# A weight's high and low part issued as two pieces of an issue model

## The chip, the cores and the metric

The kernel runs on one core of one Trainium2 chip. The metric is the device time of one execution in microseconds; the time before is the median of three runs. One further execution was recorded by the hardware profiler, and all durations below come from it.

## The reference

The reference is a small decoder trunk: two layers, each a half-step feed-forward block, a token mixer and a second half-step feed-forward block, with RMS norms before and after each. The input x is 256 tokens of 1024 values, all in float32.

```python
D_MODEL, SEQ, DEPTH, D_FF = 1024, 256, 2, 2816

def swiglu(x, w_gu, w_down):
    g, u = jnp.split(x @ w_gu, 2, axis=-1)
    return (jax.nn.silu(g) * u) @ w_down

def hybrid_mixer(h, w_in, w_out, ...):
    proj = h @ w_in
    pa, pb, pc = jnp.split(proj, [2 * A_WIDTH, 2 * A_WIDTH + B_IN], axis=-1)
    gate_a, rec_a = jnp.split(pa, 2, axis=-1)
    rec = causal_dwconv(rec_a, lru_conv_w, lru_conv_b)
    ya = rg_lru(rec, ...) * jax.nn.gelu(gate_a)      # sigmoid gates, a scan along the tokens
    yb = ssd_mixer(pb, ...)                          # decay matrices in chunks of 128 tokens
    yc = chunk_sgu(pc, ...)                          # gelu, layer norm, a 128 x 128 mixing matrix, a product
    return jnp.concatenate([ya, yb, yc], axis=-1) @ w_out
```

Nearly all of the arithmetic is in the products with the weights; the mixer has many small steps beside them.

## The kernel before

**Matmuls in three passes.** Each float32 operand is held as a high part (rounded to the format fp32r) and a low part (the remainder). A product is high·high, high·low and low·high, all accumulated in the same bank (`mm3`, `b_tile`, `wide_tile`; lines 436, 719 and 742 record the matmuls). The activations are split the same way into nT.

**Weights.** There are 656 weight units of 128 rows and up to 512 columns, used once each in a fixed order and numbered d. SP loads them in chunks of four, about 1 MB, into three buffers named stg (line 356). ACT then writes a unit's high part into a slot (a copy, line 407, or a scaled activation, line 411), and DVE writes the low part, stg minus high (line 408, or line 412 with the scale). There are 17 slots (named s_w in the profile), and a few spare ones of another kind (s_a). A slot comes free when PE has used the unit for the last time. A chunk's buffer comes free when its four low parts are written.

**What sets the order.** The program is written out by a model of time in Python: `T` holds a modelled time for each engine, and PE's is "now". PE's matmuls are issued by the main path. Everything else (evacuations, norms, convolutions, the recurrent unit, the state-space chunks, the gating unit) is a *chain*: a generator that issues one operation when the model finds it due. `Chain.op` (line 138) decides this: an operation that needs the result of another engine is due 0.13 us (`HOP`) after it, and is issued when this is at most 0.7 us (`AHEAD`) ahead of now. `pump` moves the chains that are due and then calls `fill`, which issues weight splits while a slot is free and `fill_time` is not ahead of now: that is the later of the modelled DVE time, the modelled ACT time (each less 0.6, `FILL`) and the arrival of the chunk. One call of `split_next` issues the high on ACT and the low on DVE together, and books the time of both.

Only up to 15 us of modelled time (`PIN`) is this order kept exactly; after that a scheduler places the instructions with the written order as priority. Each engine executes its own instructions in order, so an instruction that waits holds up everything behind it on its engine.

**The places touched by the steps below.** In a feed-forward block, `evac_block` takes the block sums of a row tile through a silu on ACT, a product on DVE and four transposes on PE. In the mixer, `decay` and `decay_group` build the decay matrices (sixteen PE matmuls, twelve exponentials on ACT), `sgu` is the gating unit (gelu on ACT, statistics on DVE, rstd and two products per row tile on POOL, matmuls with wst, transposes with ident), `conv` the convolutions on DVE, `lru_tile` the recurrent gates (matmuls with wbd, sigmoids on ACT), `ssd_chunk` the state-space chunks, and `post` the norm behind a block with the update of x.

Of the kernel before, what the change touches and what calls it, by code (L numbers as in the profile page):

```python
# [8 lines left out]
F32 = mybir.dt.float32  # L9
# [3 lines left out]
ALU = mybir.AluOpType  # L13
# [15 lines left out]
HOP = 0.13  # L29
# [193 lines left out]
class Kernel:  # L223
    def __init__(self, ctx, tc, x, wts, pf, pb, gpost, wst, wri, out):
# [33 lines left out]
        self.next_dma = self.next_split = 0  # L258
        self.wt, self.wh, self.wready, self.slot_time = {}, {}, {}, {}
        self.extra, self.keep_free = 0, 4  # L260
        self.pairs = {}


# [104 lines left out]
    def fill_time(self):  # L368
        d = self.next_split
        ci, _ = self.u2c[d]  # L370
        if self.slot_kind() is None or d < 2 and ("nT", 0, d, 0) not in self.ready:
            return 0.0
        return max(self.T["dve"] - FILL, self.T["act"] - FILL, self.carrive.get(ci, 0.0) - 0.3)

    def fill(self):
        did = False
        while self.next_split < len(self.units):
            d = self.next_split
# [1 line left out]
            while self.next_dma <= min(ci + NSTG - 1, len(self.chunks) - 1):  # L380
                self.dma_chunk()
            kind = self.slot_kind()
            if kind is None or d < 2 and ("nT", 0, d, 0) not in self.ready:
                break
            lead = d - self.cur
            if self.fill_time() > self.now() and (lead > 2 or self.carrive[ci] > self.now() + 0.3):
# [7 lines left out]
    def split_next(self, kind):  # L394
        d = self.next_split
        nc, T = self.nc, self.T
        u = self.units[d]
        w = unit_width(u)
        ci, o = self.u2c[d]
        src = self.ctile[ci][:, o:o + w]  # L400
        t, h = self.get([P, 2, 512], F32R, kind)
        hi, lo = t[:, 0, :w], t[:, 1, :w]
        sc = u[3] is not None
        T["act"] = max(T["act"], self.carrive[ci], self.slot_time.get(h, 0.0) + HOP) + 0.095 + w * 0.000833 + 0.095 * sc
        T["dve"] = max(T["dve"], T["act"] + HOP) + 0.07 + 0.06 * sc + w * 0.00104
        if not sc:
            self.keep(nc.scalar.copy(hi, src))  # L407
            self.keep(nc.vector.tensor_tensor(out=lo, in0=src, in1=hi.bitcast(F32), op=ALU.subtract))  # L408
        else:
            s = self.pcol(u[1], u[3][0], u[3][1])  # L410
            self.keep(nc.scalar.activation(hi, src, AF.Copy, scale=s))  # L411
            self.keep(nc.vector.scalar_tensor_tensor(out=lo, in0=src, scalar=s, in1=hi.bitcast(F32),  # L412
                                                     op0=ALU.mult, op1=ALU.subtract))
        self.wt[d], self.wh[d], self.wready[d] = t, h, T["dve"]
        self.next_split += 1

    def unit(self, d):
        self.cur = max(self.cur, d)
# [847 lines left out]
```

## Time and profile before

| what | value |
|---|---|
| median of 3 runs | 965.46 us (965.22 to 966.49) |
| profiled execution | 964.02 us, span 962.2 us, granted clock 0.998 |
| PE busy | 945.7 us, 98% of the span |
| DVE busy | 701.3 us, 73% |
| ACT busy | 622.8 us, 65% |
| POOL busy | 39.1 us, 4% |
| chain that ended last | PE 88%, DVE 7%, ACT 2% |
| low parts on DVE (lines 412 and 408) | 307.3 + 122.2 us, 623 instructions |
| high parts on ACT (lines 411 and 407) | 285.1 + 107.5 us, 623 instructions |

A row of a timeline gives the start, the time that a group of like instructions took, the engine, the line, the operation, what it writes and reads, the count, and in brackets the idle time before it with what ended it. A row of the table of stages gives a stretch of time, its length, and the busy time of PE, the weight loads of PE (PEld), DVE, ACT and POOL, then the clock, the share of the DMA engines and their rate. The rows of PE's waits give the sum of a wait, how often it came and the longest. Line 138 is the line of `Chain.op`: all chain operations have it, so they are told apart by their tiles.

### The profile page before, as it was taken

The numbers are of one execution on the slowest core, as the hardware profiler recorded it, in microseconds if no ns is written. First come the engines' busy times: TensorE is split into PE (matmuls) and PEld (weight loads), VectorE is DVE, ScalarE is ACT, GpSimd is POOL, SyncE is SP. The second block draws the span as 40 slices with busy tenths as digits, with TensorE's granted clock in tenths as the row PEclk, the third lists the DMA queues.
The fourth block names the chain that finished last, engine by engine and source line by source line (L and its number), as shares of the span: only waits on it lengthen the run. The fifth ranks groups of instructions, "written<-read, shape, count | busy, mean of one in ns | idle before, by whom it ended". The sixth has DMA issues, their size and how long they took to land.

```text
span 962.2 us, 13913 instructions
## 1 busy us (share of the span) xinstructions
PE 945.7 (98%) x5150; PEld 814.4 (85%) x5150; DVE 701.3 (73%) x1313; ACT 622.8 (65%) x1199; POOL 39.1 (4%) x58
## 2 busy tenths in 40 slices
PE   9999999999999999999999999999999999999997
PEld 7888888889987888888888888888999778888885
DVE  4997776566899777776566888666588997787732
ACT  7876665576968676665565666655589686665631
POOL 1100000001001100000010000000010100000000
PEclk9999999999999999999999999999999999999999
DMA  7865565443236755566435455663431564455621
GB/s 259 326 215 198 195 215 203 153 175 111 88 134 220 283 181 197 177 219 223 170 132 196 176 190 205 220 229 114 171 125 49 211 231 188 177 205 195 218 78 44
DMA packets 27140, 175.51 MB, mean 182 GB/s; under 512 B 3008, under 2 KB 3392, under 8 KB 8384
## 3 DMA queue, kind: packets, MB, share of 16 engines
q1 hardware_dynamic: 25200, 169.93, 49.6%
q10 hardware_dynamic: 1872, 4.70, 1.4%
q8 instruction: 40, 0.66, 0.3%
q14 instruction: 28, 0.23, 0.1%
HBM read 173.57 MB, written 1.05 MB: 181 GB/s over the span
## 4 chain that ended last, share of the span: by engine, by line
PE 88%; DVE 7%; ACT 2%; issue 1%; POOL 1%; DMA 0%; SPq 0%; DVEq 0%; POOLq 0%; ACTq 0%
PE acc L742 42%; PE acc L436 39%; PE acc L138 4%; PE acc L719 3%; DVE s_a L138 3%; DVE s_w L412 2%; ACT s_a L138 1%; DVE s_f L138 1%; DVE x L138 1%; POOL postr L138 1%; ACT L138 1%; DMA x<-in_x_dram 0%; ACT junk L138 0%; DVE s_m L138 0%; POOL lnr L138 0%
## 5 line engine op out<-in xcount | busy, mean ns | idle before, releaser
L742 PE MATMUL acc<-nT,s_w 128*128 128x512 f32 x2240 | 395.0, 337 | 0.0
L742 PEld LDWEIGHTS acc<-nT,s_w 128*128 128x128 f32 x2240 | 343.1, 188 | 48.2
L412 DVE SCALAR_TENSOR_TENSOR s_w<-stg,pf,s_w 128x512 fp32r<-128x512 f32 (+2 forms) x439 | 307.3, 735 | 54.3 <-ACT s_w L411 53.9
L411 ACT ACTIVATE s_w<-stg,pf 128x512 fp32r<-128x512 f32 (+2 forms) x439 | 285.1, 702 | 59.0 <-PE acc L436 32.6
L436 PE MATMUL acc<-s_w,s_a 128*128 128x512 f32 x984 | 227.4, 390 | 0.0
L436 PEld LDWEIGHTS acc<-s_w,s_a 128*128 128x128 f32 x984 | 184.4, 188 | 38.1
L408 DVE TENSOR_TENSOR s_w<-stg,s_w 128x512 fp32r<-128x512 f32 x184 | 122.2, 689 | 42.5 <-ACT s_w L407 42.1
L407 ACT CAST s_w<-stg 128x512 fp32r<-128x512 f32 x184 | 107.5, 619 | 52.7 <-PE acc L436 34.6
L436 PE MATMUL acc<-s_w,nT 128*128 128x512 f32 (+1 forms) x522 | 129.6, 395 | 0.8 <-DVE nT L138 0.5
L138 DVE TENSOR_TENSOR s_m<-acc,s_m 128x256 f32<-128x256 f32 (+2 forms) x172 | 71.2, 417 | 66.0 <-ACT s_m L138 61.6
L436 PEld LDWEIGHTS acc<-s_w,nT 128*128 128x128 f32 x522 | 96.0, 190 | 20.8 <-DVE s_w L412 1.5
L138 ACT COPY s_m<-acc 128x256 f32<-128x256 f32 x144 | 52.4, 364 | 83.0 <-PE acc L742 82.9
L719 PE MATMUL acc<-nT,s_w 128*128 128x256 f32 x588 | 76.0, 283 | 0.0
L719 PEld LDWEIGHTS acc<-nT,s_w 128*128 128x128 f32 x588 | 71.5, 188 | 0.3
L436 PE MATMUL acc<-s_w,s_m 128*128 128x512 f32 x192 | 48.0, 399 | 0.0
L436 PEld LDWEIGHTS acc<-s_w,s_m 128*128 128x128 f32 x192 | 35.1, 188 | 7.0
L138 DVE TENSOR_TENSOR s_f<-acc,gp 128x512 f32<-128x512 f32 x24 | 16.5, 687 | 33.3 <-ACT junk L138 33.1
L138 ACT ACTIVATE s_m<-s_m 128x512 f32<-128x512 f32 x36 | 22.7, 629 | 25.1 <-DVE s_m L138 25.1
L138 POOL TENSOR_TENSOR postr<-postv,mhalf 128x1 f32<-128x1 f32 x12 | 9.8, 819 | 693.4 <-DVE postv L138 693.4
L138 ACT ACTIVATE junk<-acc 128x512 bf16<-128x512 f32 x24 | 14.2, 594 | 35.9 <-PE acc L436 35.5
L138 ACT CAST s_a<-s_m 128x512 fp32r<-128x512 f32 x36 | 22.2, 617 | 20.7 <-DVE s_m L138 20.7
L138 DVE SCALAR_TENSOR_TENSOR s_a<-s_f,pf,s_a 128x255 f32<-128x255 f32 (+2 forms) x60 | 29.6, 502 | 4.5 <-ACT s_a L138 4.3
(138 smaller groups left out, 608.6 us busy)
## 6 DMA issues: line engine op xcount, KB each, us to landing
stg<-in_wts_dram SPq DMA_DIRECT2D x146, 1024.0 KB, 4.8
stg<-in_wts_dram SPq DMA_DIRECT2D x12, 768.0 KB, 4.2
stg<-in_wts_dram SPq DMA_DIRECT2D x4, 780.0 KB, 4.2
gp<-in_gpost_dram ACTq DMA_DIRECT2D x6, 512.0 KB, 5.5
stg<-in_wts_dram SPq DMA_DIRECT2D x3, 512.0 KB, 4.2
x<-in_x_dram SPq DMA_DIRECT2D x4, 256.0 KB, 5.1
out_dram<-x SPq DMA_DIRECT2D x4, 256.0 KB, 2.0
pb<-in_pb_dram ACTq DMA_DIRECT2D x2, 265.0 KB, 6.2
```

Source lines behind the costliest of these rows:

```text
L138: ins = fn(*args, **kw)
L407: self.keep(nc.scalar.copy(hi, src))
L408: self.keep(nc.vector.tensor_tensor(out=lo, in0=src, in1=hi.bitcast(F32), op=ALU.subtract))
L411: self.keep(nc.scalar.activation(hi, src, AF.Copy, scale=s))
L412: self.keep(nc.vector.scalar_tensor_tensor(out=lo, in0=src, scalar=s, in1=hi.bitcast(F32), op0=ALU.mult, op1=ALU.subtract))
L436: self.keep(mm(out, a, b, start=start and i == 0, stop=stop and i == 2))
L719: self.keep(self.nc.tensor.matmul(out, a, b, start=k == 0 and i == 0, stop=k == KT - 1 and i == 2))
L742: self.keep(self.nc.tensor.matmul(out, a, x, start=k == 0 and i == 0, stop=k == KT - 1 and i == 1))
```

## The change

The low part of a weight is no longer issued with its high part. `split_next` issues the high as before and adds a chain, `split_low`, that issues the low part by the rule of `Chain.op`: when its high part's modelled end plus 0.13 us is at most 0.7 us ahead of now. The modelled time of DVE is booked only then, and a unit counts as ready only when its low part has been issued. While more than two low parts are outstanding, no further high part is issued.

```diff
     def fill_time(self):
...
-        if self.slot_kind() is None or d < 2 and ("nT", 0, d, 0) not in self.ready:
+        if self.slot_kind() is None or self.lows > 2 or d < 2 and ("nT", 0, d, 0) not in self.ready:
             return 0.0
...
     def fill(self):
...
-            if kind is None or d < 2 and ("nT", 0, d, 0) not in self.ready:
+            if kind is None or self.lows > 2 or d < 2 and ("nT", 0, d, 0) not in self.ready:
                 break
...
     def split_next(self, kind):
...
         T["act"] = max(T["act"], self.carrive[ci], self.slot_time.get(h, 0.0) + HOP) + 0.095 + w * 0.000833 + 0.095 * sc
-        T["dve"] = max(T["dve"], T["act"] + HOP) + 0.07 + 0.06 * sc + w * 0.00104
+        c = Chain(self, T["act"])
+        c.eng = "act"
         if not sc:
             self.keep(nc.scalar.copy(hi, src))
-            self.keep(nc.vector.tensor_tensor(out=lo, in0=src, in1=hi.bitcast(F32), op=ALU.subtract))
+            low = c.tt(w, lo, src, hi.bitcast(F32), ALU.subtract)
         else:
             s = self.pcol(u[1], u[3][0], u[3][1])
             self.keep(nc.scalar.activation(hi, src, AF.Copy, scale=s))
-            self.keep(nc.vector.scalar_tensor_tensor(out=lo, in0=src, scalar=s, in1=hi.bitcast(F32),
-                                                     op0=ALU.mult, op1=ALU.subtract))
-        self.wt[d], self.wh[d], self.wready[d] = t, h, T["dve"]
+            low = c.stt(w, lo, src, s, hi.bitcast(F32), ALU.mult, ALU.subtract)
+        self.add(self.split_low(c, low, d, t, h))
         self.next_split += 1
+
+    def split_low(self, c, low, d, t, h):
+
+        self.lows += 1
+        yield from low
+        self.lows -= 1
+        self.wt[d], self.wh[d], self.wready[d] = t, h, c.t
```

In the changed kernel the lines of the matmuls are 444, 727 and 750, the high parts have lines 409 and 413, and the low parts have line 138 like the other chain operations. Buffer numbers differ between the two programs, since they are given in the order of issue.

**Three places where the order differs.** First ACT in the second feed-forward of layer 1 (about 320 us). Rows that write s_w or s_a from stg are the high parts of weights; the first row is d226 before and d227 after, and the row with acc and rs is the silu of row tile 1. Before:

```order
L411 ACTIVATE s_w_3332<-stg,pf 128x512
L411 ACTIVATE s_w_3338<-stg,pf 128x512
L534 DMA gp<-in_gpost_dram 128x1024
L138 ACTIVATE s_m_3345<-acc_3230,rs_3177 128x512
L411 ACTIVATE s_w_3361<-stg,pf 128x512
L138 COPY s_m_3378<-acc_3350 128x256
L411 ACTIVATE s_w_3387<-stg,pf 128x512
```

After:

```order
L413 ACTIVATE s_w_3335<-stg,pf 128x512
L413 ACTIVATE s_w_3343<-stg,pf 128x512
L413 ACTIVATE s_w_3345<-stg,pf 128x512
L542 DMA gp<-in_gpost_dram 128x1024
L138 ACTIVATE s_m_3350<-acc_3230,rs_3184 128x512
L413 ACTIVATE s_w_3372<-stg,pf 128x512
L413 ACTIVATE s_a_3374<-stg,pf 128x512
```

The silu (s_m with acc_3230) stood behind d227 and now stands behind d229, two high parts later; on DVE the two low parts likewise stand ahead of the product that follows the silu.

Second PE in the first mixer (about 225 us). Rows with later, tri and ad are the sixteen matmuls of `decay_group`; the others are tiles of the projection (`b_tile`). Before:

```order
L719 MATMUL acc_2226<-nT,s_w_2068 128x256 x3
L138 MATMUL acc_2261<-later,ident_r 128x384
L138 MATMUL acc_2261<-tri,ad 128x128 x3
L138 MATMUL acc_2262<-later,ident_r 128x384
L138 MATMUL acc_2262<-tri,ad 128x128 x3
L138 MATMUL acc_2263<-later,ident_r 128x384
L138 MATMUL acc_2263<-tri,ad 128x128 x3
L138 MATMUL acc_2265<-later,ident_r 128x384
L138 MATMUL acc_2265<-tri,ad 128x128 x3
L719 MATMUL acc_2266<-nT,s_w_2076 128x256 x3
```

After:

```order
L727 MATMUL acc_2229<-nT,s_w_2066 128x256 x3
L727 MATMUL acc_2273<-nT,s_w_2075 128x256 x3
L727 MATMUL acc_2273<-nT,s_w_2081 128x256 x3
L727 MATMUL acc_2273<-nT,s_w_2087 128x256 x3
L727 MATMUL acc_2273<-nT,s_w_2094 128x256 x3
L727 MATMUL acc_2273<-nT,s_w_2105 128x256 x3
L727 MATMUL acc_2273<-nT,s_w_2112 128x256 x3
L727 MATMUL acc_2273<-nT,s_w_2118 128x256 x2
L138 MATMUL acc_2299<-later,ident_r 128x384
L138 MATMUL acc_2299<-tri,ad 128x128 x3
L138 MATMUL acc_2307<-later,ident_r 128x384
L138 MATMUL acc_2307<-tri,ad 128x128 x3
```

The decay matmuls began with the next projection tile (acc_2266 before, acc_2273 now) and now begin 20 of its 24 matmuls later. On DVE two low parts (d168 and d169) stand ahead of the decay pieces (nacs, wdt) that feed them.

Third DVE in the same mixer (from about 231 us). bst, bmv, lnv and the TENSOR_SCALAR rows with lnr are the gating unit's layer norm; rows with s_f and pf are convolution pieces; s_w is a low part. Before:

```order
L138 TENSOR_TENSOR s_f_2334<-acc_2266,rb 128x256
L138 BN_STATS bst<-s_a_2043 128x6
L138 BN_STATS bst<-s_a_2143 128x6
L138 BN_AGGR bmv<-bst 128x2 x2
L138 TENSOR_SCALAR lnv<-bmv 128x1 x2
L138 TENSOR_SCALAR s_a_2352<-s_a_2043,bmv,lnr 128x256
L138 TENSOR_SCALAR s_a_2367<-s_a_2143,bmv,lnr 128x256
L138 SCALAR_TENSOR_TENSOR s_a_2333<-s_f_2334,pf,s_a_2333 128x255
L138 SCALAR_TENSOR_TENSOR s_a_2333<-s_f_2334,pf,s_a_2333 128x254
L138 TENSOR_TENSOR s_f_2375<-acc_2336,rb 128x256
L138 SCALAR_TENSOR_TENSOR s_a_2333<-s_f_2334,pf,s_a_2333 128x253
L412 SCALAR_TENSOR_TENSOR s_w_2513<-stg,pf,s_w_2513 128x384
```

After:

```order
L138 TENSOR_TENSOR s_f_2337<-acc_2273,rb 128x256
L138 BN_STATS bst<-s_a_2051 128x6
L138 BN_AGGR bmv<-bst 128x2
L138 SCALAR_TENSOR_TENSOR s_a_2336<-s_f_2337,pf,s_a_2336 128x255
L138 TENSOR_TENSOR s_f_2377<-acc_2340,rb 128x256
L138 SCALAR_TENSOR_TENSOR s_a_2336<-s_f_2337,pf,s_a_2336 128x254
L138 TENSOR_SCALAR lnv<-bmv 128x1
L138 BN_STATS bst<-s_a_2146 128x6
L138 SCALAR_TENSOR_TENSOR s_a_2336<-s_f_2337,pf,s_a_2336 128x253
L138 BN_AGGR bmv<-bst 128x2
L138 SCALAR_TENSOR_TENSOR s_a_2336<-s_f_2377,pf,s_a_2336 128x255
L138 TENSOR_SCALAR lnv<-bmv 128x1
```

The statistics of the second row tile (s_a_2143 before, s_a_2146 now) stood ahead of all convolution pieces and now stand between them; the low part at the end (s_w_2513) has moved further back. The second mixer, at 697 to 774 us, has the same moves.

More of the change, by code (lines that the diff above doesn't have):

```diff
@@ L260, in __init__ @@
         self.extra, self.keep_free = 0, 4
+        self.lows = 0
         self.pairs = {}
```

## The prediction

> **What bounds the kernel now.** I read the busy times first, then what PE waits for over the whole span, then a table of stages. PE rows carry the end of the program:
>
> ```profile
> PE 945.7 (98%) x5150; PEld 814.4 (85%) x5150; DVE 701.3 (73%) x1313; ACT 622.8 (65%) x1199; POOL 39.1 (4%) x58
> PE 88%; DVE 7%; ACT 2%; issue 1%; POOL 1%; DMA 0%; SPq 0%; DVEq 0%; POOLq 0%; ACTq 0%
> ...
> PE acc L138 <- DVE x L138: 3.2, 5, 0.9
> PE acc L138 <- DVE s_a L138: 2.0, 2, 1.0
> PE acc L138 <- ACT s_a L138: 1.0, 2, 0.5
> PE acc L436 <- DVE s_w L412: 0.3, 1, 0.3
> ```
>
> PE is busy 945.7 of 962.2 us, so 16.5 us is all that any order can win. The last row says what the low parts cost PE directly: it waited once for one, 0.3 us. If the change wins, it is not because weights arrive sooner. It is because DVE, on which every low part runs, does other work earlier or later. So I looked for the stages where PE idles (columns: PE busy, PEld, DVE, ACT, POOL, clock, DMA share, GB/s):
>
> ```profile
> 232.00:246.00 14.00, 13.03 (x101) 12.30 (x101) 13.15 (x35) 10.12 (x23) 4.03 (x6) 1.00 0.23 77
> 246.00:262.00 16.00, 15.34 (x129) 14.93 (x129) 13.14 (x35) 15.29 (x33) 0.00 (x0) 1.00 0.19 67
> 285.00:300.00 15.00, 13.79 (x61) 10.48 (x61) 14.27 (x29) 13.19 (x31) 2.29 (x3) 1.00 0.53 193
> ...
> 223.00:300.00 77.00, 74.08 (x496) 66.08 (x495) 67.09 (x153) 62.86 (x139) 8.30 (x11) 1.00 0.35 121
> 697.00:774.00 77.00, 74.00 (x496) 66.03 (x495) 67.00 (x153) 62.70 (x139) 8.28 (x11) 1.00 0.34 121
> ```
>
> The last two rows are the two mixers: PE idles 2.9 us in one and 3.0 us in the other, of which 0.97, 0.66 and 1.21 us lie in the three stages above them, and DVE is busy 13 to 14 us of each 14 to 16. Here DVE's order decides. In the feed-forward stages PE has no idle worth naming, so there a new order can only cost.
>
> **The change part by part.** It adds and removes no instruction: PE, DVE, ACT, POOL and SP issue as many as before, and every DMA stands in its old order. All terms are PE stalls that go or come.
>
> **Two new stalls in the feed-forward stages.** In the second feed-forward of layer 1 the block sums of row tile 1 go ACT (silu), DVE (product), PE (four transposes). The order listing shows that ACT now has the highs of two more weights (d228, d229 of the unit list) ahead of the silu, and DVE their two lows ahead of the product:
>
> ```profile
> 319.72 1.94 ACT L411 ACTIVATE s_w<-stg,pf 128x512 fp32r<-128x512 f32 x3
> 321.56 0.67 ACT L138 ACTIVATE s_m<-acc,rs 128x512 f32<-128x512 f32 x1
> 323.55 0.72 ACT L411 ACTIVATE s_w<-stg,pf 128x512 fp32r<-128x512 f32 x1 [1.32 <-DMA stg<-in_wts_dram]
> ...
> 319.85 2.74 DVE L412 SCALAR_TENSOR_TENSOR s_w<-stg,pf,s_w 128x512 fp32r<-128x512 f32 x4 [2.27 <-ACT s_w L411]
> 322.51 0.68 DVE L138 TENSOR_TENSOR s_m<-acc,s_m 128x512 f32<-128x512 f32 x1
> ...
> 321.63 1.90 PE L742 MATMUL acc<-nT,s_w 128*128 128x512 f32 x10
> 323.61 0.60 PE L138 MATMUL acc<-ident,s_m 128*128 128x128 f32 x4
> ```
>
> The high of d228 cannot start before its DMA lands, 323.55. The x3 row gives 0.61 us from one high to the next, so d229 starts at 324.16, the silu at 324.8, and it ends near 325.5 (0.67). The product (0.68) ends at 326.2 to 326.3. PE's transposes move back by nine matmuls. Eleven matmuls lie between 321.63 and 323.61, 0.18 each, so PE stands there at 323.61 + 1.6 = 325.2. What was free before (the silu done 1.3 us before that DMA) becomes a **stall of about 1.1 us**. The cover was the time in which ACT waited for the DMA; it is gone because the silu now queues behind it.
>
> The same pattern stands at 37 us in the first feed-forward, with a table load on top:
>
> ```profile
> 21.18 1.28 ACT L138 ACT_TABLE_LOAD   x1 [0.40 <-PE acc L436]
> 22.47 0.69 ACT L138 ACTIVATE s_m<-acc,rs 128x512 f32<-128x512 f32 x1
> 30.10 0.72 ACT L411 ACTIVATE s_w<-stg,pf 128x512 fp32r<-128x512 f32 x1 [1.87 <-DMA stg<-in_wts_dram]
> 30.73 1.94 ACT L411 ACTIVATE s_w<-stg,pf 128x512 fp32r<-128x512 f32 x3
> 32.57 0.67 ACT L138 ACTIVATE s_m<-acc,rs 128x512 f32<-128x512 f32 x1
> ...
> 35.72 1.03 PE L138 MATMUL acc<-ident,s_m 128*128 128x128 f32 x8
> ...
> 794.50 0.69 DVE L138 TENSOR_TENSOR s_m<-acc,s_m 128x512 f32<-128x512 f32 x1 [0.25 <-PE acc L436]
> ```
>
> The first silu, and with it the load, moves from 22.47 to behind the high of d23, which ends at 32.57. Then 1.28 for the load, 0.6 for each silu, and three highs (d24 to d26, 0.61 each) end near 37.0; the low of d26 0.66, the product 0.6, so row tile 1 is ready at 38.3. PE's transposes of tile 0 go back four matmuls and those of tile 1 one more: 35.72 + 4 × 0.18 + 0.4 + 0.18 = 37.0. **Stall 1.3 us.** The ready side hangs on the DMA of the weights (the high of d20 waits for it until 30.10 in either order), so whatever PE wins between 16 and 22 us, where the normalization's small steps move ahead of a low, is not added: it is spent here. The second layer has a move of the same kind (last row), but there the silu keeps its place and only two lows pass the product: 794.50 becomes 795.8, two thirds of which PE's own move by four matmuls (0.7) covers; the product had been ready before PE came, and I take no stall. Sum of the feed-forward stages: **+2.4 us**. Bounds: 0, if the DMA lands sooner than before by the 1.1 us, and +4.5, if at both places a further low gets in front of the product's consumer (0.66) and the DMA is as late as PE is early.
>
> **The front of each mixer.** Two lows pass the decay pieces on DVE (224 us), and PE takes the sixteen decay matmuls 20 matmuls of the f-tiles later:
>
> ```profile
> 225.17 0.34 PE L138 MATMUL acc<-later,ident_r 128*128 128x384 f32 x1
> 228.47 8.42 PE L719 MATMUL acc<-nT,s_w 128*128 128x256 f32 x70
> 241.17 0.41 PE L138 MATMUL acc<-ident,s_a 128*128 128x128 f32 x2 [0.97 <-DVE s_a L138]
> ...
> 230.94 1.27 ACT L138 ACTIVATE s_a<-acc,rs 128x512 f32<-128x512 f32 x2
> 243.54 1.28 ACT L138 ACT_TABLE_LOAD   x1
> 244.84 0.47 ACT L138 ACTIVATE s_a<-acc,pf 128x256 f32<-128x256 f32 x1
> ...
> 234.24 3.13 POOL L138 TENSOR_TENSOR s_a<-s_a,pb 128x256 f32<-128x256 f32 x4 [0.16 <-DVE s_a L138]
> ...
> 231.89 0.77 DVE L138 BATCH_NORM_STATS2 bst<-s_a 128x6 f32<-128x256 f32 x2
> 234.44 1.65 DVE L138 SCALAR_TENSOR_TENSOR s_a<-s_f,pf,s_a 128x255 f32<-128x255 f32 x2
> 236.79 1.00 DVE L412 SCALAR_TENSOR_TENSOR s_w<-stg,pf,s_w 128x384 fp32r<-128x384 f32 x1
> 238.10 0.60 DVE L412 SCALAR_TENSOR_TENSOR s_w<-stg,pf,s_w 128x384 fp32r<-128x384 f32 x1
> 251.25 1.00 DVE L138 SCALAR_TENSOR_TENSOR s_a<-s_f,pf,s_a 128x255 f32<-128x255 f32 x2 [1.88 <-ACT s_a L138]
> ```
>
> The x70 row gives 0.12 us a matmul, so 20 of them are 2.3 us: gelu starts at 233.3 instead of 230.94, the statistics at 234.0 instead of 231.89, and POOL's four products (0.78 each) run from about 237.8 to 240.8 instead of 234.24 to 237.4. Against this, the gating unit's matmuls and transposes go back on PE as well, the first by 24 matmuls (2.8 us), and the convolutions on DVE now stand ahead of four lows and of the gating pieces. Stepping the new order with these rows: PE reaches the second group of gating matmuls at 240.3 and waits for POOL until 240.9 (0.6), then the recurrent matmuls run without a break, and the transposes, which waited 0.97 in this row, find their products ready at 244.5. Stalls of 0.6 instead of some 1.6 (the 0.97, and three shorter ones from there to 245): **−1.0**. The recurrent sigmoids on ACT start near 242.9 instead of 244.84, with their table load before PE is done rather than after. The 1.88 us for which DVE waited for ACT fills with convolution, and the 0.51 us that PE waits for ACT at 261.85 goes: **−0.5**. Bounds of the two: −1.6 − 0.5 (every stall in the front gone) and +1.2 (the second rival).
>
> **The end of each mixer.** DVE works without a break from the chunk outputs to the update of x; its order now has the chunk chain ahead of four to six lows and the last sums ahead of two, but two lows instead of one between the sum of squares and the update:
>
> ```profile
> 287.62 2.07 DVE L412 SCALAR_TENSOR_TENSOR s_w<-stg,pf,s_w 128x512 fp32r<-128x512 f32 x3
> 292.20 0.75 DVE L412 SCALAR_TENSOR_TENSOR s_w<-stg,pf,s_w 128x512 fp32r<-128x512 f32 x1
> 293.38 1.42 DVE L138 SCALAR_TENSOR_TENSOR x<-s_f,postr,x 128x512 f32<-128x512 f32 x2 [0.44 <-POOL postr L138]
> ```
>
> The work on DVE up to the sum of squares is the same, so that moves only as far as DVE is ahead since the front, 2 us, of which PE is ahead 1.5. The second low costs 0.66, of which 0.44 filled a wait. So the 1.21 us of PE idle shrinks by 2.0 − 1.5 − 0.2 = 0.3 and by what the earlier chunk outputs give PE to do meanwhile; between 0 and 1.2 I take **−0.5**. Each mixer −2.0, both **−4.0**.
>
> **Sum.** +2.4 − 4.0 = −1.6 us. The profiled execution took 964.02 us (span 962.2 and 1.8 around it), so it would become 962.4. The runs shown have a median of 965.46, 1.4 above that execution; against the median it is **963.9 us**. About 0.2% (1.9 us) is what a measurement can tell from no change, so the forecast is a small gain that it can just about miss.
>
> **The rivals.** *More is won* (below 962.7): all PE idle in both mixers goes and one feed-forward stall proves covered: −5.9 + 1.3, about 960.9. For it: DVE is the engine behind three of PE's four waits there. Against: lead on DVE has to beat a PE that is early too.
>
> *The gains cancel* (965.1 to 967.4, about 966): the feed-forward stalls come, and each mixer gives back 1.3 of its 2.0 because its chain is moved, not shortened: 965.46 + 2.4 − 1.4 = 966.5. That PE idles only 0.97 and 0.66 us in the stages speaks for it. That the change does nothing, because lows still follow their highs, is excluded: the order differs.
>
> *Slower* (above 967.4): POOL's four products in the front become the late link. They now run beside the convolutions, which read s_f and s_a, and beside lows, which read stg and s_w. The rows show the price: two convolution pieces took 1.65 beside POOL (0.82 each, against 0.5 each at 251.25 with POOL idle), one low 1.00 against 0.60. If five such pieces between the statistics and the gating products take 0.35 more each, the gating products come 1.75 later and PE waits 2.2 more than the 0.6 above: each mixer +0.7 instead of −1.5 in the front. It decides from the point where the second transposes wait beyond 246. Then 965.46 + 2.4 + 2 × 0.7 = 969.3 with nothing won behind. Against it: the old order also had about 1.1 us of such slowing, so it is partly a change of place.
>
> The Trainium skill, "GPSIMD Engine Reference", section 1 (Specifications), names the cause: GpSimd shares its SBUF interfaces with VectorE and contends with instructions of VectorE that have two SBUF inputs. By that rule the slowing follows POOL to its new place, as this rival has it. The trace agrees: 1.00 against 0.60 us for the same low.
>
> **How the numbers follow.** Forecast (962.7 to 965.1, mixers −1.4 to −2.6 each) 0.42, a third of it beyond the 1.9 us; more won 0.27; cancelled 0.15, half of it within 1.9 us; slower 0.16. So faster 0.14 + 0.27 = 0.41, same 0.28 + 0.07 = 0.35, slower 0.08 + 0.16 = 0.24. The range 960.8 to 967.8 leaves the far ends of the first and the last rival out, under 0.2 together.
>
> **What would show it.** PE's waits list should have two new entries of 1.1 to 1.3 us for DVE s_m, at 37 and 325 us; gelu should start near 233 us and the first sigmoid ahead of 244; the entry for DVE s_a of 1.0 should go and one for POOL s_a of about 0.6 come; the second mixer should read like the first. The forecast is wrong if PE's idle per mixer stays at 2.9 us or if the silu of tile 1 at 325 us does not wait for the DMA.

## The result: slower, and the profile after

The changed kernel takes 971.55 us (median of four runs, 969.81 to 972.35); the kernel before took 965.39 beside it. The ratio is 1.0067, with an interval of 1.0054 to 1.008: 6.2 us slower, above the predicted 960.8 to 967.8. The profiled execution took 970.99 us with a span of 969.2, 7.0 more than before.

The busy times, from the page of the changed kernel:

```profile
PE 949.3 (98%) x5150; PEld 818.2 (84%) x5150; DVE 701.2 (72%) x1313; ACT 623.5 (64%) x1199; POOL 38.7 (4%) x58
```

PE issues the same 5150 matmuls and yet is busy 3.6 us longer (949.3 against 945.7); idle time grew by the other 3.4 us. Those are two different losses.

What PE waits for, in the changed kernel:

```profile
PE acc L138 <- DVE x L138: 5.3, 5, 2.0
PE acc L138 <- DVE s_m L138: 2.0, 1, 2.0
PE acc L138 <- POOL s_a L138: 1.2, 2, 0.6
PE acc L138 <- ACT s_a L138: 0.5, 2, 0.3
```

The entry for DVE s_a (2.0, in two waits of 1.0) is gone, POOL s_a has come with 0.6 twice, and ACT s_a is halved: that is the front of the mixers, much as forecast. The new DVE s_m is one wait of 2.0 us, not two of 1.1 to 1.3. And DVE x, the update of x behind a block, went from 3.2 to 5.3, with a longest wait of 2.0 instead of 0.9: the prediction has no such entry.

The other loss, the longer busy time, shows in the table of stages, at three stretches of 3.4 us of the changed kernel (columns as in the prediction; the eighth value is the clock):

```profile
41.10:44.50 3.40, 3.40 (x13) 2.92 (x12) 2.50 (x5) 1.84 (x4) 0.00 (x0) 0.50 0.77 266
300.50:303.90 3.40, 3.14 (x7) 2.49 (x8) 3.40 (x7) 3.40 (x8) 0.99 (x1) 0.50 0.80 260
774.90:778.30 3.40, 3.19 (x10) 2.31 (x9) 3.40 (x7) 3.40 (x9) 0.44 (x1) 0.50 0.57 188
```

and the first of them in the kernel before:

```profile
41.10:44.50 3.40, 3.40 (x21) 2.97 (x20) 3.40 (x9) 3.33 (x6) 0.00 (x0) 1.00 0.71 289
```

In each of the three the granted clock is 0.50, and 13 matmuls start in the first where 21 did. In the clock record the half clock lasts 3.41 us each time. Half of what PE is busy in it is lost: by the rows (3.40 + 3.14 + 3.19) / 2 = 4.9 us, 1.6 to 1.7 a stretch. (The busy time rose by less, 3.6. Half a microsecond of that is the tail, where the half clock took 3.1 us of the span instead of 4.1; the rest is not explained, but kernels without such a stretch range from 944.3 to 946.4.) Before, the clock was at half nowhere but in the tail. Each stretch stands just behind a wait of about 2.0 us.

**Where the time comes from, by place.** The transposes of the updated x are the same instructions in both programs, so they serve as milestones. PE's timeline before:

```profile
192.02 0.63 PE L138 MATMUL acc<-ident,x 128*128 128x128 f32 x4 [0.46 <-DVE x L138]
294.19 1.38 PE L138 MATMUL acc<-ident,x 128*128 128x128 f32 x8 [0.89 <-DVE x L138]
478.10 0.63 PE L138 MATMUL acc<-ident,x 128*128 128x128 f32 x4 [0.47 <-DVE x L138]
```

and after:

```profile
197.22 0.63 PE L138 MATMUL acc<-ident,x 128*128 128x128 f32 x4 [0.46 <-DVE x L138]
287.89 9.12 PE L444 MATMUL acc<-s_w,s_m 128*128 128x512 f32 x39
298.98 1.29 PE L138 MATMUL acc<-ident,x 128*128 128x128 f32 x8 [1.97 <-DVE x L138]
484.28 0.63 PE L138 MATMUL acc<-ident,x 128*128 128x128 f32 x4 [0.47 <-DVE x L138]
```

PE is 5.2 us late by 192 us, all of it from the first block: 2.0 for the wait at 40.58 us, 1.7 for the half clock behind it, 0.5 for a low part at 36.11 us that came late, and 0.4 for the load of x at the very start, which differs from one execution to the next. The other 0.6 is not assigned. In the mixer it makes up 1.5: its last matmul ahead of the x transposes ends at 287.89 + 9.12 = 297.01, where before it ended 0.89 ahead of 294.19, at 293.30; that is 3.7 late. Then the wait of 1.97 instead of 0.89 makes it 4.8, and the half clock with the wait for nT 6.2, which is still the lag at 478 us. The second mixer adds the rest up to 7.0.

**The first block.** The changed kernel's timeline, of ACT, DVE, PE and SP's queue:

```profile
20.55 0.34 ACTq L513 DMA_DIRECT2D pb<-in_pb_dram  x1
28.91 2.56 ACT L413 ACTIVATE s_w<-stg,pf 128x512 fp32r<-128x512 f32 x4 [4.42 <-DMA stg<-in_wts_dram]
...
36.52 0.68 ACT L138 ACTIVATE s_m<-acc,rs 128x512 f32<-128x512 f32 x1
...
39.84 1.01 DVE L138 TENSOR_TENSOR s_m<-acc,s_m 128x512 f32<-128x512 f32 x2
...
40.58 0.69 PE L138 MATMUL acc<-ident,s_m 128*128 128x128 f32 x4 [2.01 <-DVE s_m L138]
...
20.83 0.33 SPq L357 DMA_DIRECT2D stg<-in_wts_dram  x1
```

and ACT and SP's queue before:

```profile
21.82 0.33 ACTq L505 DMA_DIRECT2D pb<-in_pb_dram  x1
23.20 5.02 ACT L411 ACTIVATE s_w<-stg,pf 128x512 fp32r<-128x512 f32 x8
...
20.34 0.33 SPq L356 DMA_DIRECT2D stg<-in_wts_dram  x1
```

The table load and the first silu moved behind the highs, and the silu of row tile 1 (36.52) follows, as the prediction said. But ACT waits 4.42 us for a weight chunk that it did not wait for before: the eight highs at 23.20 run without a break, and the fifth of them, at 23.20 + 4 × 0.61 = 25.6, is the first of that chunk. It is now 28.91, 3.3 us later. Ahead of that chunk the loads of the mixer's parameters (pb, wst, wri) went out. ACT issues them, and with the table load and a silu gone from its front it reaches them at 20.55 instead of 21.82. The chunk is issued by SP at 20.83, 0.28 behind the first of them, and lands 8.0 us later; before, it was issued at 20.34, 1.5 ahead of them, and landed 4.8 us later. So everything in the prediction's sum for this place is right in kind and starts late, by 3.3 us for the first high of this chunk and by 2.0 for the data of the next, which landed at 31.97 and before at 30.01, and PE's wait is 2.0, not 1.3.

**The end of the mixer.** DVE before:

```profile
289.61 0.68 DVE L138 TENSOR_TENSOR s_f<-acc,gp 128x512 f32<-128x512 f32 x1
290.21 1.41 DVE L412 SCALAR_TENSOR_TENSOR s_w<-stg,pf,s_w 128x512 fp32r<-128x512 f32 x2
291.53 0.68 DVE L138 TENSOR_TENSOR s_f<-acc,gp 128x512 f32<-128x512 f32 x1
292.13 0.15 DVE L138 SCALAR_TENSOR_TENSOR postv<-pss 128x1 f32<-128x1 f32 x1
```

and after:

```profile
292.84 0.69 DVE L138 TENSOR_TENSOR s_f<-acc,gp 128x512 f32<-128x512 f32 x1 [0.34 <-ACT junk L138]
293.45 2.07 DVE L138 SCALAR_TENSOR_TENSOR s_w<-stg,pf,s_w 128x512 fp32r<-128x512 f32 x3
...
296.70 0.15 DVE L138 SCALAR_TENSOR_TENSOR postv<-pss 128x1 f32<-128x1 f32 x1
296.77 1.40 DVE L138 SCALAR_TENSOR_TENSOR s_w<-stg,pf,s_w 128x512 fp32r<-128x512 f32 x2
298.09 1.40 DVE L138 SCALAR_TENSOR_TENSOR x<-s_f,postr,x 128x512 f32<-128x512 f32 x2
```

From the first sum (s_f with gp) to postv it was 2.52 us with two lows in between, and is 3.86 with four, three ahead of the second sum and one behind it. Between postv and the update of x stand two lows instead of one. The first sum now waits for ACT's square sum of the block (0.34 idle, junk), which waits for PE. It could not have started earlier, whatever DVE had ready.

### The profile page after: what moved, and what is told of

It reads as the page before. It is cut to its first block, busy times and chain, and to the rows that moved or that the text cites. A ratio compares the mean times of both kernels' runs of the same rounds, so it can differ in the third digit from the quotient of the medians.

```text
span 969.2 us, 13919 instructions
## 1 busy us (share of the span) xinstructions
PE 949.3 (98%) x5150; PEld 818.2 (84%) x5150; DVE 701.2 (72%) x1313; ACT 623.5 (64%) x1199; POOL 38.7 (4%) x58
## 4 chain that ended last, share of the span: by engine, by line
PE 87%; ACT 5%; DVE 3%; DMA 2%; issue 1%; POOL 1%; SPq 0%; DVEq 0%; ACTq 0%; POOLq 0%
PE acc L750 41%; PE acc L444 40%; PE acc L138 4%; PE acc L727 3%; DMA stg<-in_wts_dram 2%; ACT s_a L138 2%; DVE s_a L138 2%; ACT s_w L413 1%; DVE s_w L138 1%; ACT L138 1%; ACT junk L138 0%; DVE s_f L138 0%; POOL s_a L138 0%; DVE x L138 0%; POOL postr L138 0%
## 5 line engine op out<-in xcount | busy, mean ns | idle before, releaser
L750 PE MATMUL acc<-nT,s_w 128*128 128x512 f32 (+1 forms) x2208 | 393.2, 338 | 0.5 <-DVE s_w L138 0.5
L138 DVE SCALAR_TENSOR_TENSOR s_w<-stg,pf,s_w 128x512 fp32r<-128x512 f32 (+2 forms) x435 | 303.0, 731 | 53.8 <-ACT s_w L413 53.5
L444 PE MATMUL acc<-s_w,nT 128*128 128x512 f32 (+1 forms) x522 | 132.2, 401 | 1.0 <-ACT nT L138 0.7
L444 PEld LDWEIGHTS acc<-s_w,nT 128*128 128x128 f32 x522 | 98.3, 195 | 21.0 <-ACT nT L138 1.3
L727 PE MATMUL acc<-nT,s_w 128*128 128x256 f32 x588 | 73.1, 281 | 0.0
L138 DVE TENSOR_TENSOR s_a<-s_m,s_a 128x512 fp32r<-128x512 f32 x36 | 24.7, 687 | 10.3 <-ACT s_a L138 10.3
```

The source lines that it names most:

```text
L138: ins = fn(*args, **kw)
L444: self.keep(mm(out, a, b, start=start and i == 0, stop=stop and i == 2))
L727: self.keep(self.nc.tensor.matmul(out, a, b, start=k == 0 and i == 0, stop=k == KT - 1 and i == 2))
L750: self.keep(self.nc.tensor.matmul(out, a, x, start=k == 0 and i == 0, stop=k == KT - 1 and i == 1))
```

## The experiments

Most kernels below are the changed kernel with the old coupled split for some of the units: where a condition on the unit's number d holds, the high and the low are issued together by the text of the kernel before. A layer has 328 units, so d % 328 is a place within a layer.

**The front of the mixer alone.** The new order only for the units 150 to 180 of each layer, which are split in the front of the mixer:

```diff
     def split_next(self, kind):
...
+        if not 150 <= d % 328 < 181:
+            T["dve"] = max(T["dve"], T["act"] + HOP) + 0.07 + 0.06 * sc + w * 0.00104
...
+            self.next_split += 1
+            return
         c = Chain(self, T["act"])
```

> Low parts issued separately only for the weights split in the front of each mixer (31 of 328 in each layer), all others with their high parts. Theory (the front wins 1 us of PE time per mixer, which the x update at the mixer's end keeps by half, because DVE sets that time; the wait for x grows from 1.0 to 1.5 us, not yet enough for the half clock): 965.1 - 1.0 = 964.1. Rival (the wait grows enough for the half clock): 965.1 + 2 x (1.7 - 0.5) = 967.5.

Measured: 962.51 us, ratio 0.9973 (0.9962 to 0.9983), 2.6 us faster for the two mixers. In the list of PE's waits, POOL s_a and ACT s_a read as in the full change (1.2, 2, 0.6 and 0.5, 2, 0.3), but the update of x does not:

```profile
PE acc L138 <- DVE x L138: 3.5, 5, 1.1
```

So the predicted gain of the front is there, 1.3 us a mixer, and the loss lies elsewhere. My expectation of 964.1 was too high: I had let the wait for x take back half of the gain, and it grew by 0.2 us at most, not to 1.5.

**The end of the mixer alone**, the condition being `not 181 <= d % 328 < 212`.

> Low parts issued separately only for the weights split behind the front of each mixer and in the beginning of the block after it (31 in each layer). Theory (DVE does the same work up to the x update, so its order there moves little): within 0.7 us of 965.1, no half-clock stretch, a wait for x of 1.0 to 1.5 us. Rival (the lows between the two sums at the mixer's end are what makes the wait 2 us): two half-clock stretches, 967.5 to 968.5.

Measured: 967.39 us, ratio 1.0023 (1.0013 to 1.0032), 2.3 us slower, and the list of waits has DVE x with 5.3, 5, 2.0, as in the full change. My own expectation, at most 0.7 us from the kernel before, falls; the rival holds. DVE of this kernel:

```profile
289.95 0.69 DVE L138 TENSOR_TENSOR s_f<-acc,gp 128x512 f32<-128x512 f32 x1 [0.28 <-ACT junk L138]
...
295.20 1.40 DVE L138 SCALAR_TENSOR_TENSOR x<-s_f,postr,x 128x512 f32<-128x512 f32 x2
```

From the first sum to the update of x it is 5.25 us, where before it was 293.38 − 289.61 = 3.77: the lows now stand behind the first sum, and count in full. The profiled execution has one stretch of half clock, behind the first of its two long waits.

**The same with no low parts in between.** To the last kernel a rule is added: from the moment the chain takes its buffer for the first sum of a mixer's end until x of that row tile is updated, no low part is issued.

```diff
     def split_low(self, c, low, d, t, h):
         self.lows += 1
+        while self.hold:
+            yield (lambda: not self.hold)
         yield from low
...
             f, h = yield from v.get([P, 512], F32, "f")
+            if t == n == 0 and nxt[2] in (2, 5):
+                self.hold = True
...
+        if t == 0:
+            self.hold = False
         if nxt != "out":
             yield from self.pre(t, nxt, halves)
```

> The kernel with separate low parts only behind the front of each mixer (967.4 us, a wait for x of 2.0 us), with one rule added: between the first sum for row tile 0 and its update of x at a mixer's end no low part is issued. On DVE that takes two low parts from between the two sums to behind the update, and two others likewise. Theory (four low parts behind the first sum, where the kernel before had two, make x late by 1.3 us, the wait 2 us and with it the half clock): wait of at most 1.0 us, no half-clock stretch, 965.1. Rival (the order elsewhere behind the front makes it): 967.4.

Measured: 964.19 us, ratio 0.9993 (0.9984 to 1.0002). DVE of this kernel:

```profile
289.04 1.41 DVE L138 TENSOR_TENSOR s_f<-acc,gp 128x512 f32<-128x512 f32 x2 [0.25 <-ACT junk L138]
290.37 0.15 DVE L138 SCALAR_TENSOR_TENSOR postv<-pss 128x1 f32<-128x1 f32 x1
...
291.62 1.41 DVE L138 SCALAR_TENSOR_TENSOR x<-s_f,postr,x 128x512 f32<-128x512 f32 x2 [0.44 <-POOL postr L138]
```

From the first sum to postv 1.33 us instead of 3.86, the longest wait for x falls to 0.7 us, and the loss of 2.3 us is gone. So the lows behind the first sum were the cause.

**The first block alone and all but it.** The new order only for d < 40 (the condition `d >= 40`), and for all other units (the condition `d < 40`).

> The reverse: only the first 40 weights have their low parts issued separately, the rest is as in the kernel before. Theory: 965.4 + 4.7 = 970.1, with one half-clock stretch near 41 us and none in the mixers. Rival: no change from before, 965.4.

> The change for all weights but the first 40, whose low parts are issued with their high parts as in the kernel before. In the changed kernel's profile PE falls 4.7 us behind between 18 and 45 us, and 1.0 and 0.7 us behind in the two mixers. Theory (stalls of 2 us or more halve PE's clock for 3.4 us, which costs 1.7 us each, and the first of three such places lies in the first block): 971.5 - 4.7 = 966.8, two half-clock stretches left, at the ends of the mixers. Rival (the lateness in the first block is only the DMA's scatter from run to run): 971.5 stays.

Measured: the first block alone 969.07 us, ratio 1.0037 (1.0024 to 1.005), 4.0 above the kernel before by the medians; all but it 966.63, ratio 1.0009 (0.9998 to 1.002), 1.5 above. The first block alone shows the late chunk again, on ACT and on PE:

```profile
28.55 2.57 ACT L426 ACTIVATE s_w<-stg,pf 128x512 fp32r<-128x512 f32 x4 [3.90 <-DMA stg<-in_wts_dram]
...
40.19 0.66 PE L138 MATMUL acc<-ident,s_m 128*128 128x128 f32 x4 [1.99 <-DVE s_m L138]
```

Its profiled execution, 967.27 us, has no stretch of half clock behind this wait; in three of its other runs the mean clock is 0.996 or 0.997, and they take 969.1 to 969.8, one at 0.999 takes 968.5. The other kernel's two waits for x have such a stretch behind both. Its runs sort by it: 964.8 to 964.9 at a mean clock of 0.996 to 0.997, 966.5 to 966.9 at 0.995 (seven of them), 968.7 at 0.993. Each step is 1.8 to 2.0 us. By the medians the parts sum to 4.0 + 1.5 = 5.5 us, and the full change lost 6.2; by the ratios they sum to 4.4 and it lost 6.5. So 0.7 to 2 us are left. In the mean clock the four runs of the full change lie 0.0053 below the 0.998 of before, the two parts 0.0006 and 0.0029; the 0.0018 between them is 1.7 us, about one stretch of half clock. That the gap is the clock's fits, and was not tested.

**The loads and the silus.** The parameter loads of a layer go out a fixed time of the model after its first block begins. In the kernel before I let those of layer 1 go out 1 us of the model earlier:

```diff
-        yield self.now() + 20.0
+        yield self.now() + (19.0 if l == 0 else 20.0)
```

> The kernel before, low parts issued with the high parts, with one number changed: the three loads of the mixer's parameters (pb, wst, wri, 0.7 MB) in the first block are released 1 us of modelled time earlier, which puts them ahead of the weight chunk of d16 in time, and as a consequence the first silu with its table load stands behind the high part of d23 as in the changed kernel. PE's order is unchanged. Theory (it is these two moves that make the first block late, not the separate low parts themselves): 2 to 5 us over the kernel before, 967.5 to 970, a stall near 38 us. Rival (low parts ahead of the products on DVE are the cause): within 1 us of 965.4.

Measured: 966.72 us, ratio 1.0016 (1.0007 to 1.0026). ACT of this kernel:

```profile
19.33 0.34 ACTq L505 DMA_DIRECT2D pb<-in_pb_dram  x1
28.58 2.57 ACT L411 ACTIVATE s_w<-stg,pf 128x512 fp32r<-128x512 f32 x4 [2.58 <-DMA stg<-in_wts_dram]
```

With the coupled split everywhere, the loads ahead of the chunk are enough to make ACT wait for it until 28.6, and this costs 1.6 us with no half clock in the profile. That lies between the two expectations: less than the 2 us at least that I gave the loads and the silu, more than the 1 us of the rival, and no long wait stands near 38 us. The order moved a little with it (the table load and the silus too went behind the late chunk), so 1.6 is the price of the loads with what the model makes of them.

In the changed kernel I let them go out later, `23.0 if l == 0 else 20.0`.

> The changed kernel with the loads of the mixer's parameters in the first block released 3 us of modelled time later; as a consequence both silus of the first block, with the table load, stand ahead of six high parts again and the loads come behind the weight chunk. Theory (the moved loads and the silu behind the high parts make the first block's 4.7 us): 971.5 - 4 = 967.5, no half-clock stretch near 41 us, two in the mixers as before. Rival (low parts ahead of the products on DVE make it): 970 to 971.5.

Measured: 967.11 us, ratio 1.0019 (1.0008 to 1.0029), 4.4 us less than the full change. Here the model put the silus of both row tiles, with the table load, ahead of the highs of the late chunk, and the loads behind it:

```profile
26.11 0.69 ACT L138 ACTIVATE s_m<-acc,rs 128x512 f32<-128x512 f32 x1
26.23 0.33 ACTq L513 DMA_DIRECT2D pb<-in_pb_dram  x1
...
37.34 0.65 PE L138 MATMUL acc<-ident,s_m 128*128 128x128 f32 x4
```

The chunk is issued at 21.13 and lands 5.1 us later, where it took 8.0 with the loads beside it. No wait is left at the transposes, and no half clock follows; the two mixers keep theirs. So nearly all of the first block's loss goes with the place of the loads and the silus: 967.1 is near the 966.6 of the kernel with the old first block. The two were not taken apart within the new order.

**PE kept busy through the long waits.** The changed kernel with transposes of the identity on PE ahead of the three waits (14 at each mixer's end, 16 in the first block), whose result nobody reads:

```diff
+    def busy(self, ps, n):
+        for _ in range(n):
+            ins = self.nc.tensor.transpose(ps[:, :P], self.ident, self.ident)
...
+            if t == q == 0 and ph in (2, 5):
+                self.busy(ps, 14)
...
+        if ph == b == 0 and t == 1:
+            self.busy(ps, 16)
```

> The changed kernel with junk transposes of the identity on PE ahead of its three long stalls: 16 (1.7 us) in the first block, 14 (1.5 us) ahead of the x transposes at the end of each mixer. They do no useful work and fill PE's idle time. Theory (the half clock after the stall is the larger part of the loss): no half-clock stretch at the three places, 971.5 - 3 x 1.6 = 966.7. Rival (the stall itself is the loss, the clock follows the idle time of other engines or nothing): the junk only fills time that was lost anyway, 971.5, or up to 4.7 more where it isn't hidden.

Measured: 967.33 us, ratio 1.0022 (1.0012 to 1.0032): 4.2 us less than the change, with 44 instructions more on PE. The transposes stand a few matmuls ahead of the wait, which is 0.5 at most for x. No half clock stands at any of the three places, and the mean clock is 0.997 to 0.999 in eight of ten runs. The wait itself is not shortened by this, since PE spends it on work for nobody, and part of it comes back behind the x transposes, where PE waits 1.19 and 1.07 us for nT (0.49 and 0.21 in the changed kernel). So of the loss more than half is the clock's. The profiled execution shows the same thing from the other side, at another place:

```profile
20.47 0.50 PE L444 MATMUL acc<-s_w,nT 128*128 128x512 f32 x1 [1.87 <-ACT s_w L413]
20.98 14.31 PE L444 MATMUL acc<-s_w,nT 128*128 128x512 f32 x53
```

Behind a wait of 1.87 us the 53 matmuls, which took 12.76 us in the profile of the changed kernel, took 14.31.

The same at the mixers alone, added to the kernel with the old first block:

> The kernel of the first experiment (first 40 weights as before, the rest changed) with 14 junk transposes (1.5 us) ahead of the x transposes at the end of each mixer; nothing else differs, DVE's order is the same. That kernel had two half-clock stretches of 3.4 us, each right behind a wait of 2.0 us for x, and took 966.6; its runs with one stretch fewer took 964.8. Theory (the half clock costs 1.7 us each and comes from PE's idle time): no such stretch, 966.6 - 2 x 1.7 = 963.2, faster than the kernel before. Rival (the stall and its aftermath would cost the same without it): 966.6.

Measured: 964.19 us, ratio 0.9991 (0.9982 to 1.0), 2.4 us less than without the transposes, and the mean clock 0.997 to 0.999 in all eleven runs. The theory had 3.4 less; the profile has no half clock at either place, so the stretches were worth 1.2 us each here, with the price of the transposes in it.

**Waits made by hand.** The kernel before, with one, two or three idle operations on POOL ahead of the norm's factor (postr) at three ends of feed-forward blocks, so that the update of x comes later; they compute a value that nobody reads.

```diff
+            for _ in range(self.lag):
+                late = self.small(1, "late")
+                self.nc.gpsimd.tensor_tensor(out=late, in0=v, in1=self.mhalf, op=ALU.pow)
```

> The kernel before with nothing moved: ahead of the rstd on POOL at the end of three blocks stand one, two and three more operations on one column, whose results nobody reads, so that the update of x and the wait of PE for it come 0.55, 1.1 and 1.65 us later (0.55 is the length of such an operation). The waits there, 0.6 us in each of the three, should become 1.2, 1.7 and 2.3. Theory (a wait of PE of 2 us or more halves the clock for 3.4 us, one of 1.1 us does not): one half-clock stretch behind the longest, perhaps one behind the middle one, 965.1 + 3.3 + 1.7 = 970.1, or 971.8 with both. Rival (the clock falls only behind idle time of a whole 3.4 us): none, 968.4.

Measured: 967.86 us, ratio 1.0037 (1.0024 to 1.005). PE's row for the longest:

```profile
669.27 0.63 PE L138 MATMUL acc<-ident,x 128*128 128x128 f32 x4 [2.01 <-DVE x L138]
```

The three waits are 0.98, 1.50 and 2.01, and were 0.46 to 0.47; that adds 3.1 us. Three runs have a mean clock of 0.998 or 0.999 and take 967.2 to 967.9, 2.5 to 3.1 above the kernel before; the other two have 0.996 and take 969.7 and 970.3, 2.4 more. The median is near the rival's 968.4 and not the 970.1 that I expected: the profiled execution, one of the three, has no half clock behind any of the waits. The two slower ones look like one stretch each, but where it stood is not recorded. So a wait of 2.0 us does not always bring the clock down; what decides it is taken up below, with the clock.

**All but the first block and the ends of the mixers**, the condition being `d < 40 or 181 <= d % 328 < 212`.

> The changed kernel with the low parts of the first 40 weights, and of the 31 behind each mixer's front, issued with their high parts; so the change in the mixers' fronts and in all feed-forward blocks but the first. Theory (in the feed-forward blocks the order of low parts moves nothing PE waits for): the same as with the fronts alone, 962.5 within 0.5. Rival (the stall of 1.1 us forecast for the second feed-forward block comes): 963.6.

Measured: 963.0 us, ratio 0.9986 (0.9977 to 0.9996). That is 1.8 us under the kernel before, where the front alone won 2.6; the intervals of the two ratios overlap, so it is not shown whether the lows of the feed-forward stages cost nothing or somewhat under a microsecond. At the second feed-forward of layer 1, where the prediction had a wait of 1.1 us, this kernel has 0.2, and the changed kernel none. On ACT of the changed kernel the last high ahead of the silu starts at 326.25 and the silu at 326.87: it still stands behind two more highs, but no high ahead of it waits for a DMA any more.

**The version put together.** The change with the first block as before and with the rule that holds the lows back at the mixers' ends:

> The changed kernel with the first 40 weights as before and the same rule at the mixers' ends. Theory (the change wins 1 us or more per mixer in the front, and loses only by the first block and by the low parts ahead of the x update): like the kernel with the change in the fronts alone, 962.5, or up to 0.7 better; no half-clock stretch. Rival (what the front wins is lost at the end in any case): 965 or more.

Measured: 962.1 us, ratio 0.997 (0.9961 to 0.998), 2.7 us faster than the kernel before: the lowest median of all, though the front alone, with 2.6, cannot be told from it. Its profiled execution has no stretch of half clock; three of its ten runs, at a mean clock of 0.996 or 0.997, take 963.5 to 964.1. PE's waits for x in it, and one more wait with what stands before it on ACT:

```profile
PE acc L138 <- DVE x L138: 2.5, 5, 0.5
...
323.90 0.72 ACT L427 ACTIVATE s_w<-stg,pf 128x512 fp32r<-128x512 f32 x1 [5.19 <-DMA stg<-in_wts_dram]
...
326.73 0.66 PE L138 MATMUL acc<-ident,s_m 128*128 128x128 f32 x4 [1.59 <-DVE s_m L138]
```

The wait for x is below the 3.2 of before. The wait for s_m of 1.59 us is the one that the prediction put at 325 us: two highs stand ahead of the silu, two lows ahead of the product, and the chunk comes late. It stayed without a fall of the clock in this execution.

## Why the prediction was wrong

**Mixer front: right in mechanism, place and size.** The gelu starts at 238.46, the first sigmoid at 248.41, PE waits 0.58 for POOL:

```profile
238.46 0.69 ACT L138 ACTIVATE s_a<-acc,rs 128x512 f32<-128x512 f32 x1
248.41 1.34 ACT L138 ACTIVATE s_a<-acc,pf 128x256 f32<-128x256 f32 x3 [0.94 <-PE acc L138]
...
246.35 1.10 PE L138 MATMUL acc<-s_a,wst 128*128 128x64 f32 x8 [0.58 <-POOL s_a L138]
```

Taking off the 5.2 us of lag this is 233.3 and 243.2, as stepped (233.3 and 242.9), and 0.58 against 0.6. Predicted −1.0 and −0.5 for each mixer; PE makes up 1.5 us up to the last matmul of the mixer, and the front alone gave 1.3. The rival in which POOL's products become the late link did not come.

**Mixer end: the step that failed in kind.** The prediction said that "the work on DVE up to the sum of squares is the same, so that moves only as far as DVE is ahead". The sum of the work is the same, but the chain has a gate in it: its first sum waits for ACT and PE. Lows ahead of the gate fill time that is idle anyway; the lows that the change moved behind it lie on the path, two of them, 0.66 each, which are the 3.86 − 2.52 = 1.3 us. So in place of −0.5 each end costs +1.1 of PE idle (1.97 against 0.89), and the end alone came to +1.15 a mixer with the clock in it. With the lows held back it is nil.

**First block: right in kind, short by a transfer.** "The high of d20 waits for it until 30.10 in either order" is the step that failed, and with it "every DMA stands in its old order": the transfers kept their order on each queue, but not between ACT's queue and SP's. The loads moved 1.3 us ahead with ACT, past the chunk on SP's queue, and the weights came later. 1.3 us became 2.0 of wait, with 0.5 more for a late low part ahead of it.

The Trainium skill, "DMA: Bandwidth & Descriptors", section "Issuing engines are not separate DMA queues", says that transfers issued by different engines end up on the same 16 DMA engines and interleave. The runs agree: small loads from ACT's queue, issued 0.28 us ahead of SP's chunk, make its transfer 8.0 us long; behind it they leave it 5.1.

**325 us: a term of +1.1 that did not come.** The silu does stand behind two more highs, but the high of d228 has its data. The prediction's lower bound (0, if the DMA lands sooner) is what happened; its condition was named and taken for the less likely. That is luck, for it hangs on the same order of transfers as the first block: the chunk of d228 goes out at 320.54, 0.47 ahead of the next parameter loads, and lands in 4.8 us, where it took 8.5 before. In the version put together the loads stand ahead of the chunk (312.65 against 314.36), it takes 9.4 us, and the forecast wait comes, at 1.59.

**The term that was missing: the clock.** No step of the sum put a price on what a wait does to the matmuls behind it: it stands there at nothing, without a reason. Behind the 2.0 us waits PE ran at half clock for 3.41 us: 4.9 us by the rows, against 7.0 by which the span grew. The transposes that only keep PE busy got 4.2 us back, so this is shown, not argued. The prediction's upper bound for its feed-forward stalls, 4.5 us, would have held the waits there; the clock stands in no bound.

The Trainium skill, "TensorE: Matmul & The Clock Gate", section "HAM oscillation — how this bites in real kernels", has the rule that gaps of PE above about 3.4 us bring the half clock; in Part 1 ("What's actually happening") it gives a window of 3413 ns that runs freely. The length agrees, 3.41 us in the clock record. The threshold does not: the rows show waits of 1.97 to 2.01 us with a half clock behind them. By the rule no wait here would have touched the clock, and the profiled execution would have been some 970.99 − 4.9 = 966.1. The measurement decides, and the record bears out fixed windows. The three stretches of the changed kernel start at 41.07, 300.48 and 774.93 us, 76 and 139 times 3.4133 us apart. The rows below are windows on this grid (columns as above): the one ahead of the changed kernel's second stretch, and the two over which the hand-made wait of 2.01 us was spread.

```profile
297.07:300.48 3.41, 1.26 (x8) 0.84 (x8) 3.41 (x6) 3.37 (x8) 0.85 (x1) 1.00 0.68 281
...
664.98:668.39 3.41, 2.28 (x11) 1.55 (x9) 1.43 (x4) 3.10 (x6) 2.54 (x4) 1.00 0.00 0
668.39:671.80 3.41, 2.52 (x16) 2.21 (x16) 3.41 (x6) 1.86 (x4) 0.00 (x0) 1.00 0.02 5
```

PE is busy 1.26 us of the first, and half clock follows; 2.28 and 2.52 of the others, and none follows. Over all profiled executions, the window ahead of each of the nine stretches has PE busy 1.26 to 1.75 us, and between the start and the tail only one other window has less than 1.82 (1.54, at the second mixer's end of the kernel with the ends alone). So what counts here is how much of a wait falls into one window. The grid lies differently against the program in each execution (by 2.7 us between the two shown), which makes it a chance beforehand. A sharp threshold these runs do not give, because of the one exception.

**The sum again.** In the trace the fronts give −3.0 us, as predicted; the ends +2.1, where −1.0 was predicted; the feed-forward stages +2.5 (2.0 and 0.5 in the first block, nothing at 325 us), where +2.4 was predicted. That the last two agree is luck, since one stall was larger and the other missing. With 0.4 for the load of x and 4.9 for the clock this is 6.9, against the 7.0 by which the span grew. So two steps turned a forecast of −1.6 into a loss: the mixer's end, 3.1 us off, and the clock, 4.9 us that stood in no term.

Of the rivals, none was this one: "slower" had the right sign by a mechanism that did not occur.

## What to carry to other kernels

When a change moves waits, price a wait of near 2 us of the matrix engine at its length plus the chance of 1.7 us for the half clock (behind eight of eleven such waits here), and read the granted clock of every run before comparing times. When an order moves work past a chain, find the operation at which the chain is held by another engine: what stands ahead of it is free, what stands behind it counts in full. And when an engine becomes free earlier, list what it issues next; a few hundred kilobytes of loads on its queue can delay the weights on another.

## What the runs showed that was not expected

In the profiled executions of the kernels here eleven waits of PE of 1.97 to 2.01 us stand before an x or s_m transpose, and behind eight of them the clock is at half for 3.41 us: all three of the full change, two of two in the kernel without the first block's change and in the one with the later loads, one of two in the kernel with the mixers' ends alone, none in the first block alone and in the waits made by hand, where the wait lay across two windows (2.32 and 2.50 us busy in the one, 2.28 and 2.52 in the other). Waits up to 1.6 us at such places had none; one of 1.87 us for a weight had. The kernel before, whose longest wait of this kind is 1.0, was not free of it: of its runs beside these experiments, 68 at a mean clock of 0.998 or 0.999 have a median of 964.9 us, and eight at 0.996 have 966.9, one stretch more. That is a scatter of 1.9 us, as large as most effects here, and it is read off the mean clock. No profile of such an execution of the kernel before was kept, so where its stretch stands is open.
